# A decoder trunk on one core: the first weights loaded in pieces on another queue, and the DeltaNet's side work moved two units along

## The chip, the core and the metric

The kernel runs on one core of a Trainium2 chip. A core has TensorE (PE in the profile; its weight loads are listed as PEld), VectorE (DVE), ScalarE (ACT), GpSimd (POOL) and SyncE (SP), which work side by side and wait for each other through semaphores. Sixteen DMA engines move data between the main memory and the on-chip memory SBUF. The metric is the time of one execution on the device in microseconds (us); lower is better.

## What is computed

Two decoder layers on 512 tokens of width 1024, all in float32. Layer 0 mixes tokens with a gated DeltaNet, layer 1 with a Conformer convolution; each layer then attends to a fixed memory of 256 tokens and applies an MLP of width 4096. The part of the reference that the change touches is the beginning, layer 0's norm, its projections and the DeltaNet, and the keys of the memory:

```python
def rms_norm(x, g):
    y = xf * lax.rsqrt(jnp.mean(xf * xf, axis=-1, keepdims=True) + RMS_EPS)
    return (y * g.astype(jnp.float32)).astype(x.dtype)

def gated_deltanet(h, w_in, w_conv, a_log, dt_bias, out_norm, w_out):
    proj = h @ w_in
    qkv = jax.nn.silu(causal_depthwise_conv(qkv, w_conv))
    q = l2_normalize(q) * (DN_HEAD_DIM ** -0.5)
    k = l2_normalize(k)
    beta = jax.nn.sigmoid(b_raw)
    g = -jnp.exp(a_log) * jax.nn.softplus(a_raw + dt_bias)
    o = chunk_gated_delta_rule(q, k, v, g, beta)
    o = o * lax.rsqrt(jnp.mean(o * o, axis=-1, keepdims=True) + RMS_EPS) * out_norm
    return (o * jax.nn.silu(z)).reshape(B, S, DN_INNER) @ w_out

def memory_cross_attention(h, mem_h, w_q, w_kv, w_o):
    q = (h @ w_q).reshape(B, S, XA_HEADS, XA_HEAD_DIM)
    kv = (mem_h @ w_kv).reshape(B, M, 2, XA_HEADS, XA_HEAD_DIM)
...
```

`proj` has 1024 columns each for q, k, v and z, and then 8 + 8 for b and a. The delta rule solves a triangular system per chunk of 64 tokens and head and carries a state from chunk to chunk.

## The kernel before, in words

**Matmuls in three parts.** Every weight and every activation is cut into a high part, a cast to the type float32r, and a low part, what the cast lost. A product is then three matmuls, high·high, high·low and low·high (`mm3`, lines 227 to 231). Weights come in tiles of 128 × 1024 (512 KB). `wload` issues the load of one on SP's queue (line 196); `wsplit` (lines 199 to 216) casts the high part on ACT (line 207, tile `wh`) and subtracts on DVE or, for some tiles, GpSimd (line 212, shown as line 70, tile `wl`). `wnext` (217) hands out the next tile, loads up to four ahead and casts up to two ahead (`NW = 3` buffers).

**The start.** SP's queue loads the norm gains (`prm`, line 103), the 16 columns of a and b (`wab`, 105), the first weight tile (`raw0`, 107) and the eight tiles of x (99). Meanwhile PE runs `WARM` dummy matmuls (117, 118). ACT and DVE cut `wab` (1244, 1245), the first weights (`wsplit()`, 1246) and the eight tiles of x (`n0.parts`, 1249; lines 314 and 316). Then `mm_ab` (1258 to 1265) computes the first head's k projection and, in the same loop over eight k's, the a and b columns: five matmuls for each k.

**Units.** The DeltaNet's phase is a list of main steps, run one after another on PE: a step is half of a projection (`halves`, 241), twelve matmuls. The order is k, q, z, v for heads 0 to 3, then the same for heads 4 to 7, then the 16 units of the memory's keys and values (`kv_unit`, main steps 66 to 81) and eight steps of the first half of the output projection (`do_first`, 82 to 89). Everything else hangs on this list as side work: `S.at(i, rank, f)` puts `f` behind main step `i`. The positions are constants at the end of the file: `T_STAT` for the norm's statistics (`stat`, 328; `spread`, 343, which puts 1/rms of each token into `rb`), `T_DEC` for the decay, `K2` and `Q2` for the chunk matrices of each head, `FS` for the forward substitution on DVE, `MG` for the merging of the 32 × 32 blocks, `TAPV` for v's convolution, `REC` for the recurrences of heads 0 to 3 and 4 to 7, `ONORM` for the output norm and `HO` for the transposition of the first four heads' output (`head_out`, 751). The remaining heads are transposed after the list, ahead of the second half of the output projection.

The list gives priorities: the framework orders each engine's instructions by it and by what it reckons to be ready, except for those that `tc.keep_in_program_order` pins to the order in which they are written.

Of the kernel before, what the change touches and what calls it, by code (L numbers as in the profile page):

```python
# [38 lines left out]
def tile_trunk(ctx, tc, xT, memT, prm_d, adt_d, bdw_d, tap_d, fin_d, w_ab, w_kq, w_v, w_z, w_dno, w_pw1, w_pw2,  # L39
               w_q, w_k, w_vv, w_o, w_up, w_dn, yT):  # L40
    nc = tc.nc
    pe, act, dve, pool = nc.tensor, nc.scalar, nc.vector, nc.gpsimd

    cp = ctx.enter_context(tc.tile_pool(name="cp", bufs=1))
    wp = ctx.enter_context(tc.tile_pool(name="wp", bufs=2))
# [20 lines left out]
    def const(shape, s, dt=F32):  # L66
        return cp.tile(list(shape), dt, tag=s, name=s)

    def tt(e, o, a, b, op):
        return e.tensor_tensor(out=o, in0=a, in1=b, op=op)  # L70

    def stt(o, a, s, b, op0, op1):
        dve.scalar_tensor_tensor(out=o, in0=a, scalar=s, in1=b, op0=op0, op1=op1)  # L73

    def ts(e, o, a, s1, op0, s2=None, op1=None):
        if op1 is None:
# [4 lines left out]
    def c4(t):  # L81
        return t.rearrange("p (c i) -> p c i", c=4)
# [9 lines left out]
    def pc(name, i=0):  # L92
        return prm[:, OFF[name] + i:OFF[name] + i + 1]

    def load_x():
        r = []
        for t in range(KT):
            h = slot(s="x")
            nc.sync.dma_start(out=h, in_=xT[t * P:(t + 1) * P, :])
            r.append(h)  # L100
        return r

    nc.sync.dma_start(out=prm[:, 0:NVEC], in_=prm_d[:, 0:NVEC])
    wab = slot(s="wab")[:, 0:P]
    nc.sync.dma_start(out=wab, in_=w_ab)
    raw0 = wp.tile([P, 1024], F32, tag="raw", name="raw0", bufs=NRAW)
    nc.sync.dma_start(out=raw0, in_=w_kq[0][:, 0:1024])
    xin = load_x()
    adt = const([P, 16], "adt")


# [2 lines left out]
    ones = const([P, P], "ones")  # L114
    pool.memset(ones, 1.0)
    warm = psum("warm")
    for i in range(WARM):
        pe.matmul(warm[:, 0:P], ones, ones, start=True, stop=True)
# [47 lines left out]
    for kind, gq in DN_ORDER:  # L166
        for i in range(2):
            j = gq * 2 + i
# [20 lines left out]
    ws = {"next": 0, "split": 0, "load": 1, "raw": {0: raw0}, "hl": {}}  # L189
# [9 lines left out]
    def wsplit():  # L199
        u = ws["split"]  # L200
        ws["split"] += 1
        while ws["load"] <= u:
            wload()
        raw = ws["raw"].pop(u)
        h = wp.tile([P, 1024], F32R, tag="wh", name=nm("wh"), bufs=NW)
        lo = wp.tile([P, 1024], F32R, tag="wl", name=nm("wl"), bufs=NW)
        ins = [act.copy(h, raw)]  # L207
        if u < 4:
            tc.keep_in_program_order(ins[0])
        (kind, i, *j), hf = order[u]  # L210
        gp = kind == "pw1" and 2 * i + hf > 6 or j and kind in "KV" and i == 1 and hf == 0
        ins.append(tt(pool if gp else dve, lo, raw, h.bitcast(F32), ALU.subtract))
        if u < 4:
            tc.keep_in_program_order(ins[1])
        ws["hl"][u] = (h, lo)
# [11 lines left out]
    def mm3(ps, wk, xk, first, last):  # L227
        (wh, wl), (xh, xl) = wk, xk
        pe.matmul(ps, wh, xh, start=first, stop=False)  # L229
        pe.matmul(ps, wh, xl, start=False, stop=False)  # L230
        pe.matmul(ps, wl, xh, start=False, stop=last)  # L231

    def wk(w, k):
        c = slice(k * P, (k + 1) * P)
        return w[0][:, c], w[1][:, c]
# [67 lines left out]
    class Norm:  # L303
# [5 lines left out]
            self.parts(t, h)  # L309
            self.square(h)  # L310

        def parts(self, t, h):
            xh = slot(F32R, "xh")
            act.activation(xh, h, AF.Copy, scale=pc(self.g, t))  # L314
            xl = slot(F32R, "xl")
            stt(xl, h, pc(self.g, t), xh.bitcast(F32), ALU.mult, ALU.subtract)
            self.xs.append((xh, xl))

        def square(self, h):
# [8 lines left out]
        def stat(self):  # L328
            ps = psum("ssq")
            for c in range(4):  # L330
                cs = slice(c * P, (c + 1) * P)
                pe.matmul(ps[:, c:c + 1], self.acc[:, cs], ones[:, 0:1], start=True, stop=True)
            sd = small(4, "sd")
            act.activation(sd, ps[:, 0:4], AF.Sqrt, bias=eps_rms, scale=1.0 / 1024)
            self.tok = small(4, "rstd")
            dve.reciprocal(self.tok, sd)
            if self.two:
                self.dg = diag2(self.tok, 4)
                return
            self.dg = slot(s="dg")  # L340
            tt(dve, c4(self.dg), over_c(ident), over_i(self.tok), ALU.mult)
# [476 lines left out]
    KV = {}  # L818
# [422 lines left out]
    nc.sync.dma_start(out=adt, in_=adt_d.partition_broadcast(P))  # L1241
    abp = slot(F32R, "abp")[:, 0:2 * P]
    ab3 = abp.rearrange("p (k x) -> p k x", k=KT)
    act.copy(ab3[:, :, 0:16], wab.rearrange("p (k x) -> p k x", k=KT))
    tt(dve, ab3[:, :, 16:32], wab.rearrange("p (k x) -> p k x", k=KT), ab3[:, :, 0:16].bitcast(F32), ALU.subtract)
    wsplit()
    n0 = Norm("dn_norm", dve, False)
    for t in range(KT):
        n0.parts(t, xin[t])
    D = DeltaNet(n0)  # L1250
    mains, S = [], Sides()
    at = {}
# [5 lines left out]
    def mm_ab():  # L1258
        w = wnext(("k", 0), 0)
        D.ps["ab"], D.ps["k", 0] = psum("ab"), psum("h")  # L1260
        for k in range(KT):
            mm3(D.ps["k", 0], wk(w, k), n0.xs[k], k == 0, k == KT - 1)
            xh, xl = n0.xs[k]
            pe.matmul(D.ps["ab"][0:32, :], abp[:, 32 * k:32 * k + 32], xh, start=k == 0, stop=False)
            pe.matmul(D.ps["ab"][0:16, :], abp[:, 32 * k:32 * k + 16], xl, start=False, stop=k == KT - 1)

    mains.extend([mm_ab, lambda: None, lambda: None, lambda: None])
# [20 lines left out]
    S.at(0, 3, wsplit)  # L1288
    S.at(0, 2, squares, SQ0, 8)
    S.at(T_STAT, 0, n0.stat)  # L1290
    S.at(T_STAT + 2, 0, n0.spread)
    for h in range(8):
        uk = max(at["k", h] + 1, T_STAT + 2)
# [6 lines left out]
    S.at(T_STAT + 3, 0, D.gates)  # L1300
    S.at(T_STAT + 3, 1, D.decay_const, 0)
# [141 lines left out]
NRAW = 3  # L1443
PRE = ((2, 4), (2, 6))
DN_ORDER = (("k", 0), ("q", 0), ("z", 0), ("v", 0), ("k", 1), ("q", 1), ("z", 1), ("v", 1))
LAG = (0, 0, 1)
WARM = 13
SQ0 = 8
T_STAT = 2
T_DEC = 12  # L1450
NW = 3
CONV_K, CONV_Q, CONV_V = 0, 1, (1, 1, 0, 0, 1, 1, 0, 0)
DEC1 = (37, 43)
K2 = (14, 13, 16, 17, 43, 44, 47, 46)
Q2 = (16, 18, 20, 21, 46, 48, 48, 51)
FS = ((20, 9), (50, 8))
MG = (34, 67)
V2 = (8, 8)
MGAIN = 12
ONORM = (72, 87)  # L1460
HO = 76
REC = (42, 74)
MEM = 50
MSQ = 14
TAPV = (35, 36, 37, 38, 68, 68, 69, 70)
# [104 lines left out]
```

## Time and profile before

| | us |
|---|---|
| median of 3 runs | 1531.64 (1530.73 to 1531.87) |
| the profiled execution | 1532.58 |
| span in its profile, first to last instruction | 1530.9 |
| TensorE busy | 1511.2 |
| VectorE busy | 899.1 |
| ScalarE busy | 678.8 |
| GpSimd busy | 221.8 |

A row of the timeline is: start, length, engine and line, operation, what it writes and reads, how many instructions are merged into it, and in brackets how long the engine had been idle before and what ended that. A row of the waits is: who waited, for whom, us in total, how often, and the longest. Line 70 is the helper `tt` and line 73 the helper `stt`, so there the tile's name tells the operation. A matmul's printed length overlaps the next one's; their starts tell the pace. The granted clock is the share of full speed that PE was given.

### The profile page before, as it was taken

The page shows a single profiled execution, that of the slowest core. Times are in us where ns is not written, and L with a number is a line of the kernel's source. Part 1 is how long each engine was busy: PE and PEld are TensorE (multiplying, and loading weights), DVE is VectorE, ACT ScalarE, POOL GpSimd, SP SyncE. Part 2 cuts the span into 40 slices and gives each one's busy share as a digit, 9 for nine tenths or more (in the row PEclk, how much of TensorE's full clock was granted, in tenths as well). Part 3 has the DMA queues.
Part 4 walks back from the last instruction along what each step waited for, and adds up shares of the span by engine and source line. Part 5 has one row for each costly group of instructions (what it writes and reads, how often), then busy time and mean ns, then how long its engine had stood idle before and what let it go on. Part 6 is the DMA issues. An engine that isn't in the chain of part 4 may idle for free.

```text
span 1530.9 us, 19362 instructions
## 1 busy us (share of the span) xinstructions
PE 1511.2 (99%) x7560; PEld 1274.2 (83%) x7560; DVE 899.1 (59%) x1360; ACT 678.8 (44%) x1094; POOL 221.8 (14%) x231
## 2 busy tenths in 40 slices
PE   9999999999999999999999999899999999999998
PEld 7888888988888888888888889888888888888886
DVE  6898898766545543443445699774554543434441
ACT  6847655655434442332324564464444441323332
POOL 1421220103112000000002486411111000000000
PEclk9999999999999999999999999999999999999999
DMA  5221123342213222222224524432212222222221
GB/s 182 99 84 60 61 75 111 124 149 85 72 40 110 92 100 97 96 97 97 97 98 161 169 96 136 140 132 90 79 45 96 97 96 97 98 98 97 99 105 55
DMA packets 49051, 153.56 MB, mean 100 GB/s; under 512 B 6208, under 2 KB 8000, under 8 KB 48960
## 3 DMA queue, kind: packets, MB, share of 16 engines
q1 hardware_dynamic: 48960, 152.33, 28.3%
q8 instruction: 59, 0.97, 0.2%
q14 instruction: 32, 0.26, 0.1%
HBM read 149.42 MB, written 2.10 MB: 99 GB/s over the span
## 4 chain that ended last, share of the span: by engine, by line
PE 79%; DVE 2%; ACT 1%; issue 0%; DVEq 0%; ACTq 0%
PE up L229 8%; PE up L231 8%; PE up L230 8%; PE dn L231 7%; PE dn L229 7%; PE dn L230 7%; PE pw L229 3%; PE pw L230 3%; PE pw L231 3%; PE q L229 2%; PE xo L230 2%; PE q L231 2%; PE q L230 2%; PE xo L231 2%; PE xo L229 2%; PE cv L1161 1%
## 5 line engine op out<-in xcount | busy, mean ns | idle before, releaser
L207 ACT CAST wh<-raw 128x1024 fp32r<-128x1024 f32 x248 | 260.0, 1051 | 620.9 <-PE dn L230 194.8
L70 DVE TENSOR_TENSOR wl<-raw,wh 128x1024 fp32r<-128x1024 f32 x231 | 285.9, 1239 | 109.2 <-ACT wh L207 107.7
L229 PE MATMUL up<-xh,wh 128*128 128x512 f32 x512 | 199.4, 389 | 0.0
L231 PE MATMUL up<-xh,wl 128*128 128x512 f32 x512 | 199.2, 389 | 0.0
L230 PE MATMUL up<-xl,wh 128*128 128x512 f32 x512 | 199.2, 389 | 0.0
L231 PE MATMUL dn<-uh,wl 128*128 128x512 f32 x448 | 174.3, 389 | 0.0
L229 PE MATMUL dn<-uh,wh 128*128 128x512 f32 x448 | 174.3, 389 | 0.0
L230 PE MATMUL dn<-ul,wh 128*128 128x512 f32 x448 | 174.3, 389 | 0.0
L70 DVE TENSOR_TENSOR h<-dn,h 128x512 f32<-128x512 f32 x56 | 41.8, 747 | 165.3 <-PE dn L231 165.3
L73 DVE SCALAR_TENSOR_TENSOR rl<-up,rb 128x512 f32<-128x512 f32 x64 | 44.2, 691 | 153.2 <-PE up L231 153.2
L70 POOL TENSOR_TENSOR sq<-sq,sq 128x512 f32<-128x512 f32 x30 | 48.4, 1613 | 468.6 <-ACT sq L321 468.6
L231 PEld LDWEIGHTS up<-xh,wl 128*128 128x128 f32 x512 | 96.1, 188 | 20.1
L230 PEld LDWEIGHTS up<-xl,wh 128*128 128x128 f32 x512 | 96.1, 188 | 20.1
L229 PEld LDWEIGHTS up<-xh,wh 128*128 128x128 f32 x512 | 96.1, 188 | 19.7
L230 PEld LDWEIGHTS dn<-ul,wh 128*128 128x128 f32 x448 | 84.1, 188 | 17.6
L231 PEld LDWEIGHTS dn<-uh,wl 128*128 128x128 f32 x448 | 84.1, 188 | 17.4
L229 PEld LDWEIGHTS dn<-uh,wh 128*128 128x128 f32 x448 | 84.1, 188 | 17.4
L73 DVE SCALAR_TENSOR_TENSOR ca<-x,prm,ca 128x512 f32<-128x512 f32 x112 | 82.2, 752 | 3.5 <-ACT ca L1093 1.3
L229 PE MATMUL h<-xh,wh 128*128 128x512 f32 x192 | 77.2, 402 | 1.4 <-ACT xh L314 1.4
L230 PE MATMUL h<-xl,wh 128*128 128x512 f32 x192 | 75.6, 394 | 0.6 <-DVE xl L73 0.6
L231 PE MATMUL h<-xh,wl 128*128 128x512 f32 x192 | 75.5, 393 | 0.0
L73 DVE SCALAR_TENSOR_TENSOR cva<-cv,prm,cva 128x512 f32<-128x512 f32 x60 | 49.4, 840 | 11.8 <-POOL cva L70 10.7
(354 smaller groups left out, 3065.4 us busy)
## 6 DMA issues: line engine op xcount, KB each, us to landing
raw<-w_up SPq DMA_DIRECT2D x64, 512.0 KB, 3.4
raw<-w_dn SPq DMA_DIRECT2D x64, 512.0 KB, 3.4
raw<-w_pw SPq DMA_DIRECT2D x24, 512.0 KB, 3.4
raw<-w_kq SPq DMA_DIRECT2D x16, 512.0 KB, 3.5
raw<-w_k SPq DMA_DIRECT2D x16, 512.0 KB, 3.8
raw<-w_vv SPq DMA_DIRECT2D x16, 512.0 KB, 3.4
raw<-w_q SPq DMA_DIRECT2D x16, 512.0 KB, 3.4
raw<-w_o SPq DMA_DIRECT2D x16, 512.0 KB, 3.4
```

Of the source, the lines that this page charges most:

```text
L70: return e.tensor_tensor(out=o, in0=a, in1=b, op=op)
L73: dve.scalar_tensor_tensor(out=o, in0=a, scalar=s, in1=b, op0=op0, op1=op1)
L207: ins = [act.copy(h, raw)]
L229: pe.matmul(ps, wh, xh, start=first, stop=False)
L230: pe.matmul(ps, wh, xl, start=False, stop=False)
L231: pe.matmul(ps, wl, xh, start=False, stop=last)
L1161: pe.matmul(o, x, TAPS[m][2 * j + u // 4][:, (u % 4) * P:(u % 4 + 1) * P], start=u == 0, stop=False)
```

## The change

1. *Loads.* The first weight tile is loaded in four pieces of 256 columns by DMAs that ScalarE issues. On SP's queue x's first tile now follows the gains, then `wab`, then the other seven tiles of x.
2. *Casts.* The first weights are cut in four pieces, ACT and DVE alternating with the cutting of x: a piece, two tiles of x, the next piece, and so on; `wab` is cut behind x's first tile. All these instructions, and the statistics' matmuls, are pinned. `mm_ab` multiplies high·high, low·high, a and b by x's high part, then high·low, and a and b by x's low part.
3. *Positions.* `WARM` falls from 13 to 11. The DeltaNet's side work moves two units along; the statistics move by three, the second recurrence, its output norm and `HO` by one.
4. *GpSimd.* The low half of every first half of a key tile is computed on GpSimd in both layers; before, in layer 1 only. In layer 0 these are four tiles.

```diff
-    def load_x():
+    def load_x(then=None):
...
             nc.sync.dma_start(out=h, in_=xT[t * P:(t + 1) * P, :])
             r.append(h)
+            if then and t == 0:
+                then()
...
+    raw0 = wp.tile([P, 1024], F32, tag="raw", name="raw0", bufs=NRAW)
+    for i in range(4):
+        act.dma_start(out=raw0[:, i * 256:(i + 1) * 256], in_=w_kq[0][:, i * 256:(i + 1) * 256])
     wab = slot(s="wab")[:, 0:P]
-    nc.sync.dma_start(out=wab, in_=w_ab)
-    raw0 = wp.tile([P, 1024], F32, tag="raw", name="raw0", bufs=NRAW)
-    nc.sync.dma_start(out=raw0, in_=w_kq[0][:, 0:1024])
-    xin = load_x()
+    xin = load_x(lambda: nc.sync.dma_start(out=wab, in_=w_ab))
...
-        gp = kind == "pw1" and 2 * i + hf > 6 or j and kind in "KV" and i == 1 and hf == 0
+        gp = kind == "pw1" and 2 * i + hf > 6 or j and (kind == "K" or kind == "V" and i == 1) and hf == 0
...
-                pe.matmul(ps[:, c:c + 1], self.acc[:, cs], ones[:, 0:1], start=True, stop=True)
+                ins = pe.matmul(ps[:, c:c + 1], self.acc[:, cs], ones[:, 0:1], start=True, stop=True)
+                if not self.two:
+                    tc.keep_in_program_order(ins)
...
+    for i in range(4):
+        s = slice(i * 256, (i + 1) * 256)
+        pin(act.copy(hl0[0][:, s], raw0[:, s]))
+        pin(tt(dve, hl0[1][:, s], raw0[:, s], hl0[0][:, s].bitcast(F32), ALU.subtract))
+        for k in (2 * i, 2 * i + 1):
+            n0.parts(k, xin[k], pin)
+            if k == 0:
+                wab3 = wab.rearrange("p (k x) -> p k x", k=KT)
+                pin(act.copy(ab3[:, :, 0:16], wab3))
+                pin(tt(dve, ab3[:, :, 16:32], wab3, ab3[:, :, 0:16].bitcast(F32), ALU.subtract))
     wsplit()
...
-            mm3(D.ps["k", 0], wk(w, k), n0.xs[k], k == 0, k == KT - 1)
-            xh, xl = n0.xs[k]
+            (xh, xl), (wh, wl), ps = n0.xs[k], wk(w, k), D.ps["k", 0]
+            pe.matmul(ps, wh, xh, start=k == 0, stop=False)
+            pe.matmul(ps, wl, xh, start=False, stop=False)
             pe.matmul(D.ps["ab"][0:32, :], abp[:, 32 * k:32 * k + 32], xh, start=k == 0, stop=False)
+            pe.matmul(ps, wh, xl, start=False, stop=k == KT - 1)
             pe.matmul(D.ps["ab"][0:16, :], abp[:, 32 * k:32 * k + 16], xl, start=False, stop=k == KT - 1)
...
-    S.at(T_STAT + 2, 0, n0.spread)
+    S.at(T_STAT + 1, 0, n0.spread)
...
-WARM = 13
+WARM = 11
-T_STAT = 2
-T_DEC = 12
+T_STAT = 5
+T_DEC = 14
-K2 = (14, 13, 16, 17, 43, 44, 47, 46)
-Q2 = (16, 18, 20, 21, 46, 48, 48, 51)
-FS = ((20, 9), (50, 8))
-MG = (34, 67)
+K2 = (16, 15, 18, 19, 45, 46, 49, 48)
+Q2 = (18, 20, 22, 23, 48, 50, 50, 53)
+FS = ((22, 9), (52, 8))
+MG = (36, 69)
-ONORM = (72, 87)
-HO = 76
-REC = (42, 74)
+ONORM = (74, 88)
+HO = 77
+REC = (44, 75)
```

`DEC1`, `V2` and `TAPV` move by two as well; `gates` and `decay_const` follow the spread by one unit, as before.

More of the change, by code (lines that the diff above doesn't have):

```diff
@@ L72, in stt @@
     def stt(o, a, s, b, op0, op1):
-        dve.scalar_tensor_tensor(out=o, in0=a, scalar=s, in1=b, op0=op0, op1=op1)
+        return dve.scalar_tensor_tensor(out=o, in0=a, scalar=s, in1=b, op0=op0, op1=op1)
     def ts(e, o, a, s1, op0, s2=None, op1=None):
@@ L310, in add, with parts @@
             self.square(h)
-        def parts(self, t, h):
+        def parts(self, t, h, pin=lambda i: i):
             xh = slot(F32R, "xh")
-            act.activation(xh, h, AF.Copy, scale=pc(self.g, t))
+            pin(act.activation(xh, h, AF.Copy, scale=pc(self.g, t)))
             xl = slot(F32R, "xl")
-            stt(xl, h, pc(self.g, t), xh.bitcast(F32), ALU.mult, ALU.subtract)
+            pin(stt(xl, h, pc(self.g, t), xh.bitcast(F32), ALU.mult, ALU.subtract))
             self.xs.append((xh, xl))
@@ L1243, in tile_trunk @@
     ab3 = abp.rearrange("p (k x) -> p k x", k=KT)
-    act.copy(ab3[:, :, 0:16], wab.rearrange("p (k x) -> p k x", k=KT))
-    tt(dve, ab3[:, :, 16:32], wab.rearrange("p (k x) -> p k x", k=KT), ab3[:, :, 0:16].bitcast(F32), ALU.subtract)
+    n0 = Norm("dn_norm", dve, False)
+    hl0 = wp.tile([P, 1024], F32R, tag="wh", name="wh0", bufs=NW), wp.tile([P, 1024], F32R, tag="wl", name="wl0", bufs=NW)
+    ws["split"], ws["hl"][0] = 1, hl0
+    ws["raw"].pop(0)
+    pin = tc.keep_in_program_order
+    for i in range(4):
[8 more added lines that the diff above has]
+                pin(tt(dve, ab3[:, :, 16:32], wab3, ab3[:, :, 0:16].bitcast(F32), ALU.subtract))
     wsplit()
-    n0 = Norm("dn_norm", dve, False)
-    for t in range(KT):
-        n0.parts(t, xin[t])
     D = DeltaNet(n0)
@@ L1290, in tile_trunk @@
     S.at(T_STAT, 0, n0.stat)
-    S.at(T_STAT + 2, 0, n0.spread)
+    S.at(T_STAT + 1, 0, n0.spread)
     for h in range(8):
-        uk = max(at["k", h] + 1, T_STAT + 2)
+        uk = max(at["k", h] + 1, T_STAT + 1)
         for u, ev, d, key, lag in ((uk, D.ev_k, D.KT, h, LAG[0]), (at["q", h] + 1, D.ev_q, D.M, ("q", h), LAG[1]),
@@ L1299, in tile_trunk @@
         S.at(at["z", "g", gq] + 7, 4, D.ev_z, gq)
-    S.at(T_STAT + 3, 0, D.gates)
-    S.at(T_STAT + 3, 1, D.decay_const, 0)
+    S.at(T_STAT + 2, 0, D.gates)
+    S.at(T_STAT + 2, 1, D.decay_const, 0)
     S.at(T_DEC - 2, 2, D.decay_sums)
@@ L1446 @@
 LAG = (0, 0, 1)
-WARM = 13
+WARM = 11
 SQ0 = 8
-T_STAT = 2
-T_DEC = 12
+T_STAT = 5
+T_DEC = 14
 NW = 3
 CONV_K, CONV_Q, CONV_V = 0, 1, (1, 1, 0, 0, 1, 1, 0, 0)
-DEC1 = (37, 43)
-K2 = (14, 13, 16, 17, 43, 44, 47, 46)
-Q2 = (16, 18, 20, 21, 46, 48, 48, 51)
-FS = ((20, 9), (50, 8))
-MG = (34, 67)
-V2 = (8, 8)
+DEC1 = (39, 45)
+K2 = (16, 15, 18, 19, 45, 46, 49, 48)
+Q2 = (18, 20, 22, 23, 48, 50, 50, 53)
+FS = ((22, 9), (52, 8))
+MG = (36, 69)
+V2 = (10, 10)
 MGAIN = 12
-ONORM = (72, 87)
-HO = 76
-REC = (42, 74)
+ONORM = (74, 88)
+HO = 77
+REC = (44, 75)
 MEM = 50
 MSQ = 14
-TAPV = (35, 36, 37, 38, 68, 68, 69, 70)
+TAPV = (37, 38, 39, 40, 70, 70, 71, 72)
 MLP_ORDER = [("up", 0), ("up", 1), ("dn", 0), ("up", 2), ("dn", 1), ("up", 3), ("dn", 2), ("dn", 3)]
```

## The prediction

> **What bounds the kernel now.** I read the head of the profile page first, then the waits of TensorE, with its busy time in stretches, then the timeline of the places where it waits.
>
> ```profile
> span 1530.9 us, 19362 instructions
> ...
> PE 1511.2 (99%) x7560; PEld 1274.2 (83%) x7560; DVE 899.1 (59%) x1360; ACT 678.8 (44%) x1094; POOL 221.8 (14%) x231
> ```
>
> TensorE (PE) is busy for 1511.2 of 1530.9 us. The diff adds and removes no matmul but two dummy ones, so it can only work on the 19.7 us in which PE is idle, on the dummy work at the start, and on stretches in which PE is clocked down. The largest idle stretch, in the Conformer, is touched by nothing in the diff, but it tells what a long wait costs (length, busy time of PE, PEld, DVE, ACT and POOL, then the granted clock, DMA share and GB/s):
>
> ```profile
> 970.00:1020.00 50.00, 45.20 (x241) 38.79 (x240) 40.74 (x72) 29.53 (x45) 11.11 (x5) 0.93 0.39 137
> ```
>
> PE stands for 4.8 us there, and the clock's mean of 0.93 over 50 us means 7.0 us at half speed. The diff moves the DeltaNet's schedule; PE's waits from 20 to 360 us (total, times, longest), where that runs, are:
>
> ```profile
> PE vn L692 <- DVE r L73: 1.9, 2, 1.6
> PE S L705 <- DVE vnd L70: 1.2, 1, 1.2
> PE K L231 <- DVE wl L70: 0.8, 1, 0.8
> PE ai L529 <- ACT cva L489: 0.4, 1, 0.4
> PE dt L464 <- DVE L L73: 0.4, 1, 0.4
> PE vt L644 <- ACT cva L489: 0.3, 1, 0.3
> PE do L230 <- DVE ol L73: 0.2, 1, 0.2
> ```
>
> These add to 5.2 us. What the change can win is therefore a few us, at the start; what it can lose is more of these waits.
>
> **The start, step by step.** Timeline rows (start, length, engine), first of SP's queue, then of ACT, DVE and PE, then one row of the DMA view (KB, us from issue to landing):
>
> ```profile
> 0.80 0.38 SPq L103 DMA_DIRECT2D prm<-prm  x1
> 1.25 0.41 SPq L105 DMA_DIRECT2D wab<-w_ab  x1
> 1.71 0.43 SPq L107 DMA_DIRECT2D raw<-w_kq  x1
> 2.18 4.34 SPq L99 DMA_DIRECT2D x<-xT  x8
> ```
>
> ```profile
> 3.41 0.30 ACT L1244 CAST abp<-wab 128x128 fp32r<-128x128 f32 x1 [1.02 <-DMA wab<-w_ab]
> 6.20 1.04 ACT L207 CAST wh<-raw 128x1024 fp32r<-128x1024 f32 x1 [2.50 <-DMA raw<-w_kq]
> 7.15 5.24 ACT L314 ACTIVATE xh<-x,prm 128x512 fp32r<-128x512 f32 x8
> ```
>
> ```profile
> 8.42 5.38 DVE L73 SCALAR_TENSOR_TENSOR xl<-x,prm,xh 128x512 fp32r<-128x512 f32 x8
> ```
>
> ```profile
> 1.20 5.30 PE L118 MATMUL warm<-ones 128*128 128x128 f32 x26 [1.20 <-POOL ones L115]
> 7.92 0.49 PE L229 MATMUL h<-xh,wh 128*128 128x512 f32 x1 [1.42 <-ACT xh L314]
> 8.26 0.40 PE L1264 MATMUL ab<-xh,abp 128*32 128x512 f32 x1
> 9.22 0.79 PE L230 MATMUL h<-xl,wh 128*128 128x512 f32 x1 [0.57 <-DVE xl L73]
> ```
>
> ```profile
> x<-xT SPq DMA_DIRECT2D x2, 256.0 KB, 4.8
> ```
>
> The loads stand in one queue: parameters (48 KB), w_ab (64), the first weights (512), then x. ACT's casts wait for two of them: w_ab, issued at 1.25, is there at 3.4, the weights, issued at 1.71, at 6.2. The first x tile, issued at 2.18, lands 4.8 later, at 7.0. So 112 KB are there at 3.4, 624 at 6.2, 880 at 7.0.
>
> Now x's first tile has only the 48 KB ahead on its own queue, but shares the engines with the weights on ScalarE's. Between one and all four pieces go along, so it lands when 432 to 816 KB have: between those points this is 5.1 to 6.8 us, and 6.1 for equal shares (608 KB). As x is also issued 0.93 us earlier, I take 5.8. ACT's four issues, by SP's rows 0.4 us each from about 0.8 on, are over by 2.5; they and what they push back fall into the 1.02 and 2.50 us in which ACT stood and waited for loads. From the start of ACT's xh to the first matmul are 0.77 us (7.15 to 7.92): the **first real matmul** comes at 6.6 (5.9 to 7.6), 1.3 earlier.
>
> The two parts of this first block, before and after its clock recovered:
>
> ```profile
> 7.90:12.68 4.78, 4.19 (x10) 2.43 (x11) 4.78 (x8) 4.78 (x8) 0.00 (x0) 0.64 1.05 393
> 12.68:19.60 6.92, 6.92 (x31) 4.59 (x30) 6.30 (x10) 4.82 (x9) 0.00 (x0) 1.00 0.33 128
> ```
>
> From 12.68 on, the last six of the eight k's, of five matmuls each, take 6.92 us: 0.231 a step, 1.15 per k. The first ten matmuls took 4.76 (from 7.92) instead of 2.31: 2.45 were lost to the wait for xl (0.57) and to a slow clock, whose mean of 0.64 over 4.78 us means 3.4 us at half.
>
> That came after PE had stood for 1.42 and 0.57 us in short order. Now the 11 dummies end 0.8 earlier (26 passes in 5.30, two each), at 5.7, and the gap to 6.6 is 0.9. Then wh·xh and wl·xh run, and the ab matmul waits for xl (0.67) and abp's low half (an estimated 0.3, as the small copies), some 0.75 in all. Idle 1.65 in that stretch instead of 2.0; elsewhere an idle 1.58 left the clock at 1.00:
>
> ```profile
> 170.00:180.00 10.00, 8.42 (x47) 7.02 (x46) 8.00 (x21) 7.24 (x13) 3.54 (x12) 1.00 0.08 27
> ```
>
> I take a full clock, nearer to that row, at 6 to 4. The block then ends at 6.6 + 8 × 1.15 + 0.75 = 16.6 instead of 19.6: **3.0 us won**. With x at its late bound and a slow clock (3.4 us at half cost 1.7) it ends at 19.3, 0.3 won; with x at its early bound and only 0.3 of wait, 4.2.
>
> The Trainium skill, page "TensorE: Matmul & The Clock Gate", section "What's actually happening", lets the clock fall after an idle window of about 3.4 us. By that rule the 0.9 us gap never brings it down and 3.0 stands; the trace speaks against so wide a margin, as two short gaps in one such stretch sufficed.
>
> Casting in quarters costs ACT and DVE about 0.5 us more each (128 columns cost 0.30 and 1024 cost 1.04, so each of three more instructions adds 0.19). Per two k's ACT then needs 0.4 + 2 × 0.66 and DVE as much, 1.7 us, under PE's 2.3, so it is hidden; x arrives every 0.66 us, faster than PE eats it. Without that cover 0.5 would show.
>
> **The DeltaNet, two units on.** A unit is half a projection, twelve matmuls, 2.75 us. Statistics now come after one whole projection instead of at once. Before, they and the spread matmul, one unit later, ended like this:
>
> ```profile
> 24.41 0.59 ACT L350 COPY rb<-rb 128x512 f32<-128x512 f32 x1 [0.34 <-PE rb L348]
> ```
>
> So rb, which every later DeltaNet step needs, was there at 25.0. That was 5.4 us behind the first block's end at 19.6. Now it is a projection more, 16.6 + 5.5 + 5.4 = 27.5. PE is 3.0 us earlier, the DeltaNet's side work up to 2.5 us later. Where these meet is unit 66, the memory's K matmuls:
>
> ```profile
> 250.49 4.72 DVE L596 COPY x<-TB 32x128 f32<-32x128 f32 x16
> 255.24 0.69 DVE L70 TENSOR_TENSOR cv<-h,rb 128x512 f32<-128x512 f32 x1
> 255.85 1.22 DVE L70 TENSOR_TENSOR wl<-raw,wh 128x1024 fp32r<-128x1024 f32 x1
> ```
>
> ```profile
> 250.66 6.93 ACT L596 COPY u<-UB 32x128 f32<-32x128 f32 x16 [2.01 <-DVE UB L579]
> ```
>
> ```profile
> L70 POOL TENSOR_TENSOR wl<-raw,wh 128x1024 fp32r<-128x1024 f32 x17 | 40.7, 2402 | 27.6 <-ACT wh L207 27.6
> ```
>
> K's second low half (255.85) stands behind the end of the forward substitution and its copies, and PE waits 0.8 for it. Four low halves of layer 0 go to GpSimd: 4 × 1.22 off DVE, 2.40 each on an engine that is busy for 14% of the span. Two units of lookahead (5.5 us) hide 2.40 plus the 1.05 cast. Moving the substitution two units back in the list lets the second K's cast go ahead of these copies; the block then falls on later K's, half of them GpSimd's. I take the DeltaNet's waits as unchanged at 5.2 (0 us), with bounds of 2.9 less (K, S, vt, do and part of vn gone) and 4.4 more (below).
>
> The second recurrence is one unit on: 2.75 later in the list, 3.0 earlier by PE, so nearly its old time. Behind it:
>
> ```profile
> 345.56 3.55 POOL L70 TENSOR_TENSOR z<-z,sm 128x512 f32<-128x512 f32 x3 [53.29 <-DVE sm L746]
> ...
> 352.60 1.91 PE L755 MATMUL ogT<-ident,z 128*128 128x128 f32 x16
> ```
>
> The gated output is normalised by 349.1 and PE, busy with four units of other work till then, comes for it at 352.6: 3.5 us to spare. One unit less of cover leaves 0.75, so nothing is late yet. The pins, the reordered matmuls and the helpers' return values issue nothing.
>
> **Sum.** 1532.58 us for the profiled execution (span 1530.9 and 1.7 around it) − 3.0 + 0 = 1529.6. It lies 0.9 above the median 1531.64, so I forecast **1528.6**.
>
> **Rivals.**
> 1. *The start's gain is given back* (25%, 1529.6 to 1532.5). Either the clock falls (1.7 back, 1530.3), or ScalarE's queue does not bring x any sooner (landing at 6.8, 1.0 less, 1529.6; both, 1531.3), or the second K's cast waits as before while PE comes 3.0 earlier (1531.6). For: DVE is the late one there, and a gap of 0.9 stays. Against: that wait is only 0.8 now.
> 2. *The K block costs more than the start wins* (11%, 1534.7 to 1536). Place: the second K matmul of layer 0. If the copies still go ahead of its cast, PE comes 3.0 earlier and they end 2.5 − 1.2 later: the wait grows by 4.3, past the 4.8 that took the Conformer's clock down; half a clock for 3.4 to 7.0 us costs 1.7 to 3.5. 1531.6 − 3.0 + 4.3 + 1.7 to 3.5 = 1534.6 to 1536.4. It decides once that wait exceeds about 3 us. Against: the list order above.
> 3. *GpSimd stops DVE* (5%, 1537.0). While GpSimd works, DVE stretches; a row of GpSimd and three of DVE from the K stage:
>
> ```profile
> 269.65 2.52 POOL L70 TENSOR_TENSOR cva<-cva,cvq 128x512 f32<-128x512 f32 x2 [11.85 <-ACT cvq L482]
> ```
>
> ```profile
> 270.98 1.75 DVE L73 SCALAR_TENSOR_TENSOR cva<-cv,prm,cva 128x512 f32<-128x512 f32 x1 [3.11 <-POOL cva L70]
> 272.65 0.68 DVE L70 TENSOR_TENSOR kf<-K,mrs 128x512 f32<-128x512 f32 x1
> 273.25 1.40 DVE L73 SCALAR_TENSOR_TENSOR cva<-cv,prm,cva 128x512 f32<-128x512 f32 x2
> ```
>
> The same operation takes 1.75 while the second of two GpSimd additions runs and 0.70 a moment later. If each GpSimd half stops DVE for its whole 2.40, the first K's delays DVE by 1.2 instead of freeing 1.2, and the wait of rival 2 grows by 6.7: 1531.6 − 3.0 + 6.7 + 1.7 = 1537.0. Against: it needs rival 2's order as well. The Trainium skill, page "SBUF — State Buffer", section "Who interferes with whom", has it as a rule: a VectorE instruction with two SBUF inputs and a GpSimd one that reads SBUF exclude each other. The stretched row agrees.
> 4. *The DeltaNet's waits shrink too* (14%, 1525.5 to 1527): 3.0 and up to 2.9 more, 1525.7, if GpSimd's relief frees DVE ahead of K and the second recurrence.
>
> **The numbers.** The forecast holds 45% (1527 to 1530). About 0.2% (3.1 us) is what a measurement of this kernel tells from no change, 1528.6: the forecast lies on that bound. Half of it and a little more (27 of 45) lies below, with rival 4 that makes 0.41 faster; the rest of it with rival 1 makes 0.43 same; rivals 2 and 3 are the 0.16 slower. The range leaves out rivals 2 and 3 and the outermost of 4: 1525.8 to 1533.5.
>
> **What would show it.** Right: first real matmul at 5.9 to 7.6, granted clock 1.00 from 9 to 12.5, L1265's last matmul near 16.4, rb near 27.5, waits of PE from 20 to 360 us near 5, the transposes ogT with no wait before them. Wrong: a clock of 0.50 in the start; a wait of PE at K above 3 us; DVE's low halves stretched beside GpSimd's; a wait before ogT.

## The result and the profile after

The changed kernel takes 1543.84 us (median of 5 runs, 1542.69 to 1545.47), the kernel before 1531.64 beside it (5 runs, 1529.98 to 1532.27). The ratio is 1.0082, with a 95% interval of 1.0071 to 1.0093: about 12.5 us **slower**, where a little faster was forecast. The same kernel's executions differ by a few us; most of that goes with the granted clock (0.993 in the slowest run of the changed kernel, 0.995 in the fastest).

The head of the page of the changed kernel, span and busy times:

```profile
span 1543.7 us, 19363 instructions
...
PE 1515.4 (98%) x7556; PEld 1277.4 (83%) x7556; DVE 902.3 (58%) x1359; ACT 677.4 (44%) x1097; POOL 231.6 (15%) x235
```

The span grew by 12.8 us. PE's busy time grew by 4.2 with four passes fewer, so a part of the loss is not waiting but a slower clock. Stretches of the changed kernel (length, busy time of PE, PEld, DVE, ACT, POOL, granted clock, DMA share, GB/s):

```profile
0.00:20.00 20.00, 18.55 (x80) 13.87 (x81) 11.80 (x19) 14.56 (x26) 4.77 (x22) 1.00 0.74 249
20.00:60.00 40.00, 38.10 (x180) 30.42 (x179) 33.87 (x66) 25.99 (x38) 5.91 (x10) 1.00 0.36 119
60.00:150.00 90.00, 88.67 (x507) 75.38 (x506) 74.26 (x149) 53.39 (x99) 24.39 (x44) 0.98 0.22 71
250.00:300.00 50.00, 42.92 (x350) 40.72 (x349) 39.35 (x69) 26.66 (x50) 11.58 (x12) 0.90 0.28 92
```

The same stretches of the kernel before:

```profile
0.00:20.00 20.00, 16.81 (x71) 12.53 (x71) 12.39 (x18) 13.17 (x21) 4.78 (x22) 0.91 0.64 223
20.00:60.00 40.00, 39.62 (x191) 32.20 (x192) 31.32 (x67) 28.92 (x43) 6.26 (x10) 1.00 0.35 119
60.00:150.00 90.00, 90.00 (x527) 76.55 (x527) 82.70 (x161) 55.81 (x99) 23.97 (x46) 1.00 0.21 74
250.00:300.00 50.00, 48.83 (x407) 45.83 (x406) 40.53 (x68) 34.83 (x62) 7.78 (x10) 1.00 0.35 123
```

Read by stage: the first 20 us are better, as forecast (1.7 us more work, clock 1.00 for 0.91). From 20 to 150 us PE idles 3.2 us where it idled 0.4, and the clock is down for a while. From 250 to 300 it idles 7.1 instead of 1.2, and 0.90 over 50 us is 10 us at half speed. The waits of TensorE in the changed kernel, from 20 to 370 us (total, times, longest), against those that the prediction quotes:

```profile
PE K L231 <- ACT wh L209: 6.6, 1, 6.6
PE vn L696 <- ACT cvq L486: 2.3, 1, 2.3
PE dt L468 <- DVE L L73: 1.6, 1, 1.6
PE vt L648 <- ACT cva L493: 1.4, 2, 1.2
PE ssq L547 <- ACT kt L515: 1.0, 1, 1.0
PE ogT L759 <- POOL z L70: 0.7, 1, 0.7
PE K L233 <- DVE wl L70: 0.5, 1, 0.5
```

The 5.2 us have become 14.1 in these rows. Nearly half is one wait, the 6.6 us at K. Of the rest, dt, ssq, vt and ogT were small or absent before, and vn was 1.9. The names are those of the tiles that PE writes: ct and dt belong to the decay, ai and ssq to the chunk matrices of q, mg to the merging, vt, vn, kS and S to the recurrence, ogT to the transposed output. After 370 us the two kernels run alike: the first matmul of q comes 12.1 us later than before (388.65 against 376.58), the end 12.8.

**The start** in the changed kernel: ACT, then PE's first matmul, its first wait and the last matmul of the block, then rb's copy.

```profile
5.21 0.72 ACT L316 ACTIVATE xh<-x,prm 128x512 fp32r<-128x512 f32 x1 [0.58 <-DMA x<-xT]
...
5.98 0.50 PE L1277 MATMUL h<-xh,wh 128*128 128x512 f32 x1
...
6.97 0.42 PE L1279 MATMUL ab<-xh,abp 128*32 128x512 f32 x1 [0.26 <-DVE abp L70]
...
15.74 0.39 PE L1281 MATMUL ab<-xl,abp 128*16 128x512 f32 x1
...
27.06 0.59 ACT L354 COPY rb<-rb 128x512 f32<-128x512 f32 x1 [2.76 <-PE rb L352]
```

The first block ends 3.6 us earlier (its last matmul began at 19.37 before). But rb, on which all side work of the DeltaNet hangs, is copied at 27.06 instead of 24.41, 2.7 later. At K's first matmul (256.19 against 253.02) the 3.6 us are lost and 3.2 more.

**The K stage** in the changed kernel. ACT's rows, from the cast for the second key tile to that for the fourth (and fifth):

```profile
250.72 1.06 ACT L209 CAST wh<-raw 128x1024 fp32r<-128x1024 f32 x1 [4.38 <-PE h L232]
256.16 1.05 ACT L209 CAST wh<-raw 128x1024 fp32r<-128x1024 f32 x1 [4.38 <-PE h L232]
263.80 6.67 ACT L600 COPY u<-UB 32x128 f32<-32x128 f32 x16 [6.59 <-DVE UB L583]
270.50 1.99 ACT L209 CAST wh<-raw 128x1024 fp32r<-128x1024 f32 x2
```

The casts of the second and third tile are ahead of the copies, as forecast. Then ACT stands for 6.6 us, because the next entry of its queue, the copies, waits for DVE's transposition UB; and the fourth tile's cast stands behind them and ends the wait of PE. A row of GpSimd and two of DVE from the same stage tell why the transposition is late:

```profile
246.41 2.39 POOL L70 TENSOR_TENSOR wl<-raw,wh 128x1024 fp32r<-128x1024 f32 x1 [10.17 <-ACT wh L209]
...
257.29 2.39 POOL L70 TENSOR_TENSOR wl<-raw,wh 128x1024 fp32r<-128x1024 f32 x1 [4.32 <-ACT wh L209]
```

```profile
246.11 0.40 DVE L70 TENSOR_TENSOR fst<-FT,X 128x240 f32<-128x240 f32 x1
246.55 2.52 DVE L70 TENSOR_TENSOR X<-X,fst 128x240 f32<-128x240 f32 x1
...
257.37 2.39 DVE L70 TENSOR_TENSOR fst<-FT,X 128x60 f32<-128x60 f32 x1
...
263.62 4.42 DVE L600 COPY x<-TB 32x128 f32<-32x128 f32 x16
```

Two steps of the substitution that take 0.40 and 0.22 elsewhere took 2.52 and 2.39, each as long as the GpSimd half beside it: the substitution is stopped for 4.3 us, and spared 1.22 for the one low half ahead of the copies that VectorE no longer computes. Its copies of x now begin 7.4 us after K's first matmul (263.62 and 256.19); before, 2.5 ahead of it (250.49 and 253.02).

### The profile page after: what moved, and what is told of

Same layout as the page of the kernel before. It is cut to its first block, busy times and chain, and to the rows that moved or that the text cites. A ratio compares the mean times of both kernels' runs of the same rounds, so it can differ in the third digit from the quotient of the medians.

```text
span 1543.7 us, 19363 instructions
## 1 busy us (share of the span) xinstructions
PE 1515.4 (98%) x7556; PEld 1277.4 (83%) x7556; DVE 902.3 (58%) x1359; ACT 677.4 (44%) x1097; POOL 231.6 (15%) x235
## 4 chain that ended last, share of the span: by engine, by line
PE 72%; DVE 5%; DMA 1%; ACT 1%; issue 1%; SPq 0%; POOL 0%; ACTq 0%; DVEq 0%; POOLq 0%
PE up L231 8%; PE up L232 8%; PE up L233 8%; PE dn L231 7%; PE dn L232 7%; PE dn L233 7%; DVE ca L73 4%; PE q L231 2%; PE xo L232 2%; PE q L232 2%; PE q L233 2%; PE xo L231 2%; PE xo L233 2%; PE pw L231 2%; PE pw L232 2%; PE pw L233 2%
## 5 line engine op out<-in xcount | busy, mean ns | idle before, releaser
L70 DVE TENSOR_TENSOR wl<-raw,wh 128x1024 fp32r<-128x1024 f32 (+1 forms) x230 | 280.8, 1222 | 112.9 <-ACT wh L209 106.2
L231 PE MATMUL h<-xh,wh 128*128 128x512 f32 x184 | 73.1, 397 | 0.0
L232 PE MATMUL h<-xl,wh 128*128 128x512 f32 x184 | 72.2, 392 | 0.0
L233 PE MATMUL h<-xh,wl 128*128 128x512 f32 x184 | 71.9, 391 | 0.0
L73 DVE SCALAR_TENSOR_TENSOR cva<-cv,prm,cva 128x512 f32<-128x512 f32 x60 | 49.9, 853 | 13.4 <-POOL cva L70 12.1
```

What stands on the lines that cost most here:

```text
L73: return dve.scalar_tensor_tensor(out=o, in0=a, scalar=s, in1=b, op0=op0, op1=op1)
```

## The experiments

Theories: **A**, the second substitution ends too late, so that its tail stands in ScalarE's and VectorE's queues when the key weights must be cut. **B**, GpSimd's four halves alone. **C**, the fixed order at the start disturbs what follows. **D**, the waits that the other positions bring. From the first results came **E**: the side work's chain behind rb, and not TensorE, sets the pace of the first 190 us, against **P**, TensorE's lead counts.

### One part at a time

e1 has the new start with all later positions and GpSimd as before:

```diff
-T_DEC = 14 ... FS = ((22, 9), (52, 8)) ... TAPV = (37, ...)     (and the rest)
+T_DEC = 12 ... FS = ((20, 9), (50, 8)) ... TAPV = (35, ...)
-... or j and (kind == "K" or kind == "V" and i == 1) and hf == 0
+... or j and kind in "KV" and i == 1 and hf == 0
```

> The new start (loads, casts, pins, dummies, statistics at unit 5) with every other position and GpSimd's share as before. Theory A (ScalarE's queue: the copies of the second forward substitution stand in it, wait for VectorE's substitution, and hold back the casts of K's weights; the two units and GpSimd make the substitution late): the first block ends 3.6 us earlier as in the changed kernel, the wait at K grows from 0.8 to about 3, clock 1.00 there; 1528.5 to 1531. Theory B (GpSimd's four halves alone did it by stopping VectorE): 1528 to 1529, nearly all of the 3.6 kept. Theory C (the pins of the start disturb the order of all that follows): 1535 or more, with the waits dt, ssq and vn of the changed kernel.

e2 is the changed kernel without the GpSimd halves (the second pair of lines of that diff):

> The changed kernel with GpSimd's share as before (keys of layer 0 all on VectorE). Theory A: the substitution ends some 2 us earlier, as VectorE is no longer stopped twice for 2.1 us and takes two halves of 1.2 back; the wait at K falls from 6.6 to about 4 to 5 and is still there; 1538 to 1542. Theory B: no wait at K above 1 us, 1529 to 1533. Theory C: as theory A or slower, the waits before unit 66 stay.

e3 is the kernel before with the changed positions from `T_DEC` to `TAPV`, and e4 the kernel before with GpSimd's halves:

```diff
e3: -T_DEC = 12 ... FS = ((20, 9), (50, 8)) ...     +T_DEC = 14 ... FS = ((22, 9), (52, 8)) ...
e4: -... kind in "KV" and i == 1 ...     +... (kind == "K" or kind == "V" and i == 1) ...
```

> The kernel before with only the DeltaNet's positions moved (two units, second recurrence one), old start and statistics, old GpSimd share. Theory A: the substitution ends about two units later against the projections, so a wait at K of 3 to 6 us behind ScalarE's copies and a slow clock there; 1536 to 1542. Theories B and C: 1531 to 1533.

> The kernel before with only GpSimd's four halves of layer 0's keys. Theory A: VectorE is stopped once or twice ahead of K, the copies start 1 to 2 us later, the wait at K is 0.8 to 3; 1531 to 1534. Theory B: wait of 5 or more at K and a slow clock, 1538 to 1543. Theory C: 1531 to 1532.

| kernel | median us | ratio to before (95%) | over before's 1531.16 |
|---|---|---|---|
| e1, start alone | 1534.78 | 1.0024 (1.0014 to 1.0033) | +3.6 |
| e3, positions alone | 1537.44 | 1.0044 (1.0029 to 1.0058) | +6.3 |
| e4, GpSimd alone | 1533.76 | 1.0017 (1.0008 to 1.0027) | +2.6 |
| e2, start and positions | 1538.53 | 1.0048 (1.0031 to 1.0066) | +7.4 |

The three parts add up to 12.5, the whole change cost 12.7 over this same median; that they agree is chance, since the first two cost 7.4 together (e2) and not 9.9. No part gains, the start included, which neither A nor B had expected. GpSimd's halves cost 2.6 alone and 5.3 on top of the other two (1543.84 − 1538.53), where the substitution is late already. The largest wait in e3:

```profile
PE K L231 <- DVE wl L70: 3.8, 1, 3.8
```

With the positions alone the wait at K is 3.8 us (0.8 before), and it is VectorE's low half that ends it. DVE's copies and the low halves of e3:

```profile
259.97 4.50 DVE L596 COPY x<-TB 32x128 f32<-32x128 f32 x16
264.50 2.36 DVE L70 TENSOR_TENSOR wl<-raw,wh 128x1024 fp32r<-128x1024 f32 x2
```

The second key tile, whose high part was cast at 255.14, gets its low part at 264.50, behind the copies. In e4, where the substitution is not moved, 1.0 is added at K and 0.6 at vt; the rest of its loss stands in no single wait:

```profile
PE K L231 <- DVE wl L70: 1.8, 1, 1.8
```

So B alone falls, and A stands for the K stage. The start's loss is another thing; the waits of e1:

```profile
PE mg L620 <- ACT w L610: 1.9, 1, 1.9
PE ct L446 <- DVE grep L423: 1.7, 1, 1.7
...
PE ssq L547 <- ACT sqq L535: 1.1, 1, 1.1
PE dt L468 <- DVE L L73: 0.8, 1, 0.8
PE K L233 <- DVE wl L70: 0.8, 1, 0.8
```

At K it is as before. The new waits, 5.5 us together against 0.4 before, lie at 42 to 135 us, and behind two of them the clock halves for 3.41 us, here the first of the two (its mean is the number after POOL's):

```profile
71.71:75.12 3.41, 3.41 (x9) 2.74 (x10) 3.06 (x9) 3.31 (x8) 1.84 (x5) 0.50 0.43 154
```

Together the two lose 3.4 us. The squares of x are where it begins; DVE's sums of squares, in the kernel before and then in e1:

```profile
13.72 5.46 DVE L70 TENSOR_TENSOR sq<-sq,sq 128x512 f32<-128x512 f32 x7
```

```profile
16.02 5.46 DVE L70 TENSOR_TENSOR sq<-sq,sq 128x512 f32<-128x512 f32 x7
```

The sums start 2.3 later, since the pinned low half of the second weight tile (14.88 to 16.02) goes ahead of them; rb and the side work behind it follow, while PE is 4 us earlier. By amount this is nearly C's number (1535 or more); what it is that disturbs was the next question.

### The substitution's place

f1 gives the second group of heads back its old positions, in the changed kernel:

```diff
-DEC1 = (39, 45)   K2 = (..., 45, 46, 49, 48)   FS = ((22, 9), (52, 8))   MG = (36, 69)   REC = (44, 75)   (and the rest)
+DEC1 = (37, 43)   K2 = (..., 43, 44, 47, 46)   FS = ((22, 9), (50, 8))   MG = (36, 67)   REC = (44, 74)   (and the rest)
```

> The kernel after the change with every position of the second group of heads (decays, substitution 50 in place of 52, merges, taps, recurrence, output norm) as before the change; the start, the first group's positions and GpSimd's four halves stay. Theory A (the second substitution ends two units too late, so its transposes and copies stand in DVE's and ScalarE's queues at the moment the layer-0 key weights must be split): the waits at K fall from 6.6 + 0.5 us to at most 2.5, the 10.2 us of half clock there go, and of 1543.8 about 5 + 5 us go: 1531 to 1535. Theory D (the waits that the other positions bring at 50 to 190 us, dt 1.6, ssq 1.0, vt 1.2, vn 2.3, are the loss): 1539 or more.

f2 fixes ScalarE's sixteen copies behind two more of the casts, in the changed kernel:

```diff
-        if u < 4:
+        if u < 4 or kind == "K" and j[0] == 0:
             tc.keep_in_program_order(ins[0])
-                S.at(f0 + nf, 2 - i, D.mg_a, h, i)
+                S.at(f0 + nf + gq * (1 - i) * (7 + h % 4 // 2), 2 - i, D.mg_a, h, i)
```

(The copies of heads 4 to 7 are pinned in `mg_a` in the same way.)

> The kernel after the change, but ScalarE's sixteen copies of the second substitution (u from UB) are fixed in its queue behind the casts of the fourth and fifth key tile; nothing else moves, DVE's transposes and copies stay. If ScalarE's queue alone is the cause: the wait at K falls from 6.6 us to under 1, no half clock there, 1531 to 1534. Theory A (the substitution is late on both engines; DVE's copies of x still run to about 268 and the fourth tile's low half stands behind them): K still waits 3 to 5 us, 3.4 to 6.8 us of half clock stay, 1537 to 1542.

f3 changes one number of the kernel before:

```diff
-FS = ((20, 9), (50, 8))
+FS = ((20, 9), (52, 8))
```

> The kernel before with one number changed: the second substitution begins at unit 52 in place of 50. Theory A: the wait at K grows from 0.8 to about 3.8 us (DVE's low half behind the transposes and copies) and the clock halves for 3.4 to 6.8 us there: 1533.5 to 1537.5, span 3 to 6 us over before. Theory D (the other positions cost): 1530.5 to 1532.5.

f3 took 1534.35 us (1.0023, 1.0015 to 1.0032), 3.4 over before; its one grown wait is that at K:

```profile
PE K L231 <- DVE wl L70: 2.4, 1, 2.4
```

Its copies of x, and then those of e2, where PE comes to K 4.4 us later than before:

```profile
257.93 4.57 DVE L596 COPY x<-TB 32x128 f32<-32x128 f32 x16
...
262.26 4.49 DVE L600 COPY x<-TB 32x128 f32<-32x128 f32 x16
```

By the time, two units on this one constant are half of what all positions cost (A, and D for the rest); the wait was expected at 3.8. The rest of e3's 6.3 us would then be the larger wait at K and the waits that grew at vt (0.3 to 1.4), ogT (0 to 0.7), vn (1.9 to 2.3) and dt (0.4 to 0.8).

f2 took 1542.75 us (1.0078, 1.0066 to 1.0090). Its rows of ACT and of DVE:

```profile
259.16 1.05 ACT L209 CAST wh<-raw 128x1024 fp32r<-128x1024 f32 x1 [1.97 <-PE K L232]
```

```profile
263.62 4.44 DVE L600 COPY x<-TB 32x128 f32<-32x128 f32 x16
...
268.69 2.96 DVE L70 TENSOR_TENSOR wl<-raw,wh 128x1024 fp32r<-128x1024 f32 x1
```

The fourth cast runs at 259.16, 11 us earlier than in the changed kernel, and PE still waits 6.5 us, now for the low half behind DVE's copies. ScalarE's queue was the last releaser in the profile and not the cause; taking it away gained nothing that can be told (1.0078 against 1.0082). It came out worse than A's own numbers (3 to 5 us): the low half takes 2.96 in place of 1.22 beside a GpSimd half (268.24 to 270.58), and the copies, later now, also hold up a merge (PE waits 2.9 there).

f1 took 1537.72 us (1.0040, 1.0028 to 1.0052), 6 us less than the changed kernel, 3 more than A expected and 1 less than D. Its waits at K:

```profile
PE K L233 <- POOL wl L70: 1.9, 1, 1.9
...
PE K L231 <- ACT wh L209: 1.5, 1, 1.5
```

The 7.1 us have halved, and 3.4 us at half clock are left of 10.2. The longer of the two is a wait for a GpSimd half itself: two units of lookahead do not hide it once its cast is held up.

f4 has the new start, the first group one unit on, the second group and GpSimd as before:

```diff
-T_DEC = 14   K2 = (16, 15, 18, 19, ...)   FS = ((22, 9), (52, 8))   REC = (44, 75)   (and the rest)
+T_DEC = 13   K2 = (15, 14, 17, 18, ...)   FS = ((21, 9), (50, 8))   REC = (43, 74)   (and the rest)
```

> The start of the kernel after the change, the first group's positions one unit along in place of two, the second group's as before, GpSimd as before. Theory A: the start's 3.6 us stay won except for what DVE's and ScalarE's chain of the first 150 us takes back (start alone: ct 1.7, ssq 1.1, mg 1.9 us more waits and two half-clock windows of 3.4 us), about half of it with one unit: 1528 to 1531. Rival E (the first 150 us are bound by DVE and ScalarE, so PE meets a wait of the same sum wherever the positions stand): 1531.5 to 1535.

It took 1536.71 us (1.0034, 1.0022 to 1.0046), worse than either expectation and not better than e1 (1.0014 to 1.0033): the waits at ct (1.7) and mg (1.9) are as long as in e1, that at ssq is gone, those at vt and ai are longer. Moving the side work one unit along does not catch what the start loses.

### What the start's lead is worth

g2 is the kernel before with the statistics and what hangs on them one unit later and nothing else (their sums' matmul still follows the first block, at 19.97; the spread into rb comes a unit later), g4 the same with three more dummy matmuls, g3 with the first weights on ScalarE's queue in one piece and no fixed order:

```diff
g2: -T_STAT = 2     +T_STAT = 3
g4: -WARM = 13      +WARM = 16
g3: -    nc.sync.dma_start(out=raw0, in_=w_kq[0][:, 0:1024])     +    act.dma_start(...)
```

> The kernel before with one number changed: the statistics and what hangs on them one unit later (2 to 3). TensorE's first block stays; rb's copy comes at about 27.2 us in place of 24.4, as in the changed kernel. Theory E: 2 to 4 us slower, 1533 to 1535. If the late rb costs nothing (the start alone loses by its early matmuls or its fixed order): 1530.5 to 1532.

> The kernel before with 16 warm-up matmuls in place of 13, so that TensorE has no gap before the first real matmul (1.42 us) and the clock should not halve at 9.1 to 12.5 us: TensorE is about 1.7 us ahead at 20 us, and nothing else moves. Theory E (the side work's chain sets the pace): the lead is lost again in waits before 190 us and the time is 1530.3 to 1531.5. Theory P (TensorE's lead counts): 1528.8 to 1529.8.

> The kernel before with one line changed: the first weight tile is loaded whole by a DMA that ScalarE issues, so that x's eight loads go out on SP's queue 0.5 us earlier. No order is fixed. Theory E: rb's copy moves by as much as the last tiles of x do (0 to 1.5 us earlier) and the time with it: 1529 to 1531. If ScalarE's issue (0.8 us) ahead of its table load delays its casts instead: rb later and 1531 to 1532.5.

g1 is e1 with the squares and their sums pinned ahead of the second weight tile's split, and the statistics at unit 3:

```diff
-            act.activation(sq, h, AF.Square)
+            pin(act.activation(sq, h, AF.Square))          (the sums likewise)
...
-    wsplit()                                               (ahead of the list)
+    S.at(0, 1, wsplit)                                     (behind the squares)
-T_STAT = 5
+T_STAT = 3
```

> The start alone (positions and GpSimd as before), but the squares of x and their sums are fixed ahead of the split of the second weight tile, and the statistics stand at unit 3 in place of 5. In the start alone DVE's sums of squares begin at 16.0 us (13.7 before) and the copy of rb stands at 27.0 (24.4 before), so the chain of side work behind rb is 2.6 us later while TensorE is 4 us earlier. Theory E (that chain, not TensorE, sets when the DeltaNet comes out): rb's copy is back at 24 +-1, the new waits at ct (1.7) and mg (1.9) shrink to under 0.7 each, and the time is 1529.5 to 1533 although TensorE stands 2 to 4 us at 16 to 20 us. Theory P (TensorE's lead is what counts): those 2 to 4 us come on top of the start alone's 1534.8: 1536 to 1539.

| kernel | first matmul | last of the block | rb's copy | waits at ct, dt, mg and q's ssq, sum | K's first matmul | median us, ratio (95%) |
|---|---|---|---|---|---|---|
| before | 7.92 | 19.37 | 24.41 | 0.4 | 253.02 | 1531.84 |
| g3 | 7.75 | 17.68 | 23.98 | 0.4 | 252.64 | 1531.15, 0.9999 (0.9990 to 1.0008) |
| g4 | 8.34 | 18.26 | 24.57 | 0.4 | 253.21 | 1530.97, 0.9999 (0.9990 to 1.0008) |
| g1 | 5.61 | 16.01 | 26.29 | 0.4 | 254.96 | 1533.44, 1.0009 (1.0000 to 1.0018) |
| e1 | 5.91 | 15.42 | 27.00 | 5.5 | 259.23 | 1534.78, 1.0024 (1.0014 to 1.0033) |
| g2 | 8.23 | 19.73 | 27.42 | 4.2 | 259.60 | 1536.69, 1.0035 (1.0022 to 1.0047) |

The two rows at the bottom decide. g2's first block ends about where it did before, e1's 4 us earlier; both have rb at 27, both come to K at 259 to 260, over six us late, and both wait at mg, ssq and dt. Six us late at K is not six us in the end: from the first matmul of cross-attention's q to the last instruction, e1's and g2's profiles take 1150.3 us and that of before 1154.3. In that of before, PE waits 4.2 us at once for the keys of layer 1 (up to 980.08) and has half a clock for 6.8 there; in e1's it waits 2.8, in g2's 2.5, with a full clock. These edits do not touch that place. g2's two largest waits at mg, ssq and dt:

```profile
PE mg L616 <- ACT w L606: 1.8, 1, 1.8
PE ssq L543 <- ACT sqq L531: 1.3, 1, 1.3
```

A late rb alone, with what hangs on it, costs as much as e1 lost, if not more (the intervals overlap): E. g4 tells less between E and P than it was built for. In its profile the clock does not halve in the first 20 us and the block ends 1.1 earlier than in that of before, but e3, e4 and g3, which start like before, were profiled without that drop too and end it at 17.7 to 17.9; against them g4 has no lead. What all four show is that an end of the block ahead of DVE's sums is worth nothing: PE then stands for the sums for 0.98 to 0.99 us. g4's row, and g1's, where the wait is longer:

```profile
19.65 1.05 PE L332 MATMUL ssq<-ones,sq 128*128 128x1 f32 x8 [0.99 <-DVE sq L70]
```

```profile
19.88 1.05 PE L335 MATMUL ssq<-ones,sq 128*128 128x1 f32 x8 [3.48 <-DVE sq L70]
```

g1 confirms the chain from the other side: PE stands 3.5 us for the sums, but the waits at ct, ssq and mg are gone, and it is no slower than e1 for that (1533.44 against 1534.78). It fixes the order of more instructions than e1, so a fixed order as such (C) is not what costs; it matters what stands first in it. Its rb was expected at 24 and came at 26.3, since the spread matmul stands a unit behind the statistics and PE had stood; its time is 0.4 above E's range, as g2's is 1.7 above. Where nothing is moved but the load (g3), nothing measurable is won; ScalarE's issue takes 0.40 us there and its cast of the weights is not delayed (6.04 against 6.20). No version beat the kernel before.

## Why the prediction was wrong

*The start: right.* Predicted: x's first tile at 5.8, first matmul 6.6 (5.9 to 7.6), a wait of 0.75 for abp and xl, a full clock, 3.0 us won. Measured: ACT cuts x from 5.21, first matmul 5.98, wait 0.26, clock 1.00, 3.6 won. rb was predicted at 27.5 and its copy ended at 27.65. The quarter casts stayed hidden. But, by luck, 1.7 of the 3.6 was no property of the kernel before: with the same start, e3, e4 and g3 were profiled at full clock up to 20 us, and their block's last matmul began at 17.9, 17.8 and 17.7 instead of 19.4. Against these the start wins 2 us, and so part of the sum's 3.0 was an accident of the one execution that was shown.

*The step that failed* is "I take the DeltaNet's waits as unchanged at 5.2 (0 us)". They became over 14 us, with half a clock besides. Three links of it gave way.

1. "Where these meet is unit 66." The prediction had PE 3.0 earlier and the side work 2.5 later, 5.5 us closer together, and looked for the meeting in one place only. It is met already at the decay and chunk matrices, at 42 to 135 us. There the trace of before shows waits of only 0.4, so I read slack into it; but a PE with few waits tells only that the side work comes in time, not by how much. g2, with PE as before and rb 3.0 later, and e1 show that there was no such slack, and g1 that the waits go when rb comes back towards PE.
2. "The block then falls on later K's, half of them GpSimd's." The order was right: the second cast did go ahead. But the prediction, in rival 2, let the copies end only 2.5 − 1.2 later than before, from the lateness of rb, and they began 13.1 later (263.62 against 250.49). A list position counts from PE. The two units alone put them 7.4 later (f3, with PE at K as before), and PE's lateness at K comes on top: e3, 2.2 late, and e2, 4.4 late, lie about 0.1 us from that sum. For the changed kernel, 3.2 late, it gives 261.1, and the other 2.5 are what GpSimd's halves add. The 6.93 us of copies on ACT were quoted and not costed, and the fourth tile, on DVE, stood behind 3.3 us of transpositions and 4.4 of copies as well (f2).
3. "Four low halves of layer 0 go to GpSimd", with "Two units of lookahead (5.5 us)" to hide them. Rival 3 had the mechanism: each of two halves stopped DVE for its length. Its chance of 5% came from the condition that rival 2's order must hold too; it need not. The halves fell beside the substitution, which is the late chain.

*Rival 2* came nearest in kind: 4.3 us of wait and 3.4 to 7.0 at half clock were its price, 6.6 + 0.5 and 10.2 came, at the fourth tile and not the second. *Rival 1* said that the start's gain is given back, and in e1 it is, with 3.6 us lost on top; but that was for none of its three reasons: the clock in the start was 1.00, x came sooner, and the wait at K stayed at 0.8. *Rival 4* saw nothing; GpSimd relieved DVE of four times 1.22 and stopped it for more.

*The tail.* "One unit less of cover leaves 0.75, so nothing is late yet": ogT waits 0.67, so this was off by 1.4 us. It is the smallest of the errors.

The sum afterwards, from the profile: PE's idle time up to 400 us grew by 8.4 (7.3 to 15.7, without the 1.2 ahead of the first dummy), half-speed stretches from 10.2 to 20.5 us, which is 5.1 us of lost time; 13.5 together, less some dummy matmuls, against 12.8.

## What to carry to other kernels

When the bound engine is fed by chains of side work, an earlier start of it is worth only what the chain's first link is earlier, so date the first links (here the sums of squares and rb) before counting the engine's lead. Before moving a bundle of work by a list position, work out in us what the position means at that place and whose work its tail then stands in front of on each engine; the engine that the profile names as the releaser may be only the last of two in the same position. Put work on GpSimd only where VectorE has slack for its whole length.

## What the hardware showed besides

*GpSimd and VectorE.* A VectorE operation with two SBUF operands that begins beside a GpSimd subtraction ends with it (0.40 became 2.52, 0.22 became 2.39; the rows are above). The Trainium skill, page "SBUF — State Buffer", section "Who interferes with whom", has this as a rule of exclusion, and these rows agree.

*The clock.* Its drops last 3.41 us or two or three times as much. What brings one on is not the wait's length alone. The same wait at vn, 2.30 us in the changed kernel and 2.34 in e2, left the clock alone in one and halved it in the other. Two stretches of 3.41 us of the changed kernel, then two of e2:

```profile
183.05:186.47 3.42, 2.53 (x12) 1.75 (x10) 2.32 (x8) 3.40 (x8) 2.10 (x7) 1.00 0.00 0
186.47:189.88 3.41, 2.00 (x17) 2.03 (x18) 2.04 (x5) 1.76 (x4) 1.27 (x1) 1.00 0.36 108
```

```profile
184.03:187.44 3.41, 1.36 (x7) 0.78 (x5) 3.16 (x7) 3.40 (x5) 1.09 (x6) 1.00 0.00 0
187.44:190.85 3.41, 3.12 (x15) 3.15 (x15) 0.92 (x4) 0.60 (x2) 1.27 (x1) 0.50 0.45 159
```

In all four the stretches are cut at multiples of 3.413 us from a drop of the same execution. In the changed kernel the wait falls across a boundary, and PE is busy for 2.0 us or more on either side; in e2 nearly the whole wait lies in one stretch, 1.36 busy, and the next runs at 0.50. So a drop seems to answer to the work in one stretch of a fixed grid, and where the grid lies against the kernel differs between executions: measured from the span's start, the drops of e2 and of the changed kernel are 1.0 us apart modulo 3.413. If so, executions of one kernel can differ by 1.7 us a drop. The Trainium skill, page "TensorE: Matmul & The Clock Gate", section "What's actually happening", speaks of a free-running window of 3413 ns; length and free phase agree. It has the clock fall after an idle window; here none was idle, and 1.36 us of work in 3.41 were too few. Work counted as busy is not the whole of it: a stretch of the kernel before had 1.83 us busy and no drop behind it (176.37 to 179.78), one of the changed kernel 2.38 and a drop (73.83 to 77.24), 0.91 of them matmuls of one column (ssq). With each of the fourteen profiles cut on its own grid, all drops up to 1000 us begin on the grid. If the one-column matmuls are left out, every stretch at full clock with 1.54 us of work or less was followed by half a clock, and none with 1.57 or more, but for two in g2 (1.60 and 1.72). So the border lies a little under half of the stretch in these traces; no run was made to test it.
